# One fixed order for the vector engine's attention work: index sums, choice rounds, scores and rotations queued as traced

## The chip, the cores and the metric

One core of a Trainium2 chip runs the whole program. Its engines each work through an instruction queue of their own, in order: PE (TensorE) for matrix products and transposes, DVE (VectorE) and ACT (ScalarE) for elementwise work, POOL (GpSimd) for a few small vectors, SP (SyncE) for issuing loads. The metric is device time in microseconds (us) of one execution, as the median of several runs.

## The reference

Two layers of a decoder trunk on one sequence of 256 tokens, width 1024, all in float32. Cut to what matters:

```python
for l in range(DEPTH):                               # DEPTH = 2
    mod = c_act @ w_ada[l] + b_ada[l]                # 6 x 1024: shift, scale, gate twice
    sh_m, sc_m, gt_m, sh_f, sc_f, gt_f = split(mod, 6)
    h = rms_norm(x, g_pre_mix[l]) * (1 + sc_m) + sh_m
    # token_mixer: h @ w_in, cut into q|k|v of two head groups, index q|k|weights; partial rotary on q, k
    #   group 1 (MoBA): 8 heads, plain causal attention here (one block of 256 keys)
    #   group 2 (DSA): score[t,s] = sum_h w[t,h] relu(qi[t,h] . ki[s]); the 64 best keys of each
    #                  query are kept, softmax attention over them
    #   each group's output is RMS-normed, then @ w_out
    x = x + gt_m * rms_norm(y, g_post_mix[l])
    h = rms_norm(x, g_pre_ffn[l]) * (1 + sc_f) + sh_f
    y = (gelu(conv3(h @ w_up_act)) * (h @ w_up_lin)) @ w_down
    x = x + gt_f * rms_norm(y, g_post_ffn[l])
```

## The kernel before

Every float32 weight is split on the chip into a high part (ACT, line 141, or 137 with a gain) and the rest (DVE, line 142, or 138), and each product is three passes on PE: high by high, high by rest, rest by high. The 256 tokens are two tiles of 128, called t = 0 and 1. Weights arrive as one stream of 1 MB loads on SP's queue (line 114) into six `raw` buffers, in the order in which the program asks for them.

A layer's mixer projects `ia`, `ib` (index q, index k, index weights), `mq`, `mk`, `mv`, `dq`, `dk`, `dv`, one after the other (lines 380 to 407; layer 0 opens the first four in a common start). While a projection runs, other work is laid between its matrix products by `Background`: chains of generators, each of which is advanced once per step ("tick"); a generator that yields n sleeps for n steps. One projection takes 20 steps: for each t eight, and two more for a pass that is put last (`late`). The chains:

- `T` and `D`: after the rotation of q or k (`rope_out`, lines 353 to 364: a copy on ACT, line 355, then two DVE operations, lines 359 and 364) PE transposes the heads (line 370) and ACT copies them (line 371).
- `att`: `indexer` (lines 415 to 441) multiplies index q by index k, ACT takes the relu (line 433), and DVE adds eight heads up (line 436: an index sum). Then `attend` (lines 457 to 545) for MoBA and, later, DSA: PE makes scores into banks 4 and 5, DVE adds the mask and takes the maximum (line 477: a score operation), ACT takes the exponential with its sum (line 481), DVE the reciprocal (line 484), DVE or ACT the scaling (lines 489, 487), PE transposes (line 496) and multiplies by v.
- `top0`, `top1`: `choose` (lines 443 to 453): eight rounds, each DVE's eight largest of a row (line 447) and their replacement (line 448), with `gap` steps between rounds: 3 in layer 0, 2 in layer 1. The masks that come out are needed by DSA alone.
- `sf`: `gemv_v` (lines 183 to 195): columns of the modulation by DVE, each a row product of 1024 elements with its sum (line 191), two to a load, `gap` steps between two. In layer 0 eight of them (columns 24 to 32) at a gap of 6 start with `mv`, and eight more (columns 32 to 40) at a gap of 9 follow in the same chain, added when `dq` starts.
- `gt`: four-column blocks of the modulation on PE.
- `out`: `group_out` (lines 547 to 567): a norm through PE (line 551), DVE (line 553), POOL (line 555, a power), a transpose on PE (line 558), and two DVE operations (lines 562, 564).

The program's text order is not yet the order of the queues. The framework lays each engine's instructions out at compile time: of those that its own model of the chip holds ready, the one that was traced first. So an instruction traced later may stand earlier in its engine's queue, where the earlier one was not thought ready. `tc.keep_in_program_order` and `tc.issue_after` bind single instructions; nothing of the sort binds those of lines 359, 364, 436, 447, 448 and 477.

Of the kernel before, what the change touches and what calls it, by code (L numbers as in the profile page):

```python
# [14 lines left out]
OP = mybir.AluOpType  # L15
# [11 lines left out]
FILL = -1.0e38  # L27
MARK = -3.0e38
# [46 lines left out]
def trunk(ctx: ExitStack, tc, plan, x, c, stream, small, rope, out):  # L75
    nc = tc.nc
# [7 lines left out]
    bg = Background()  # L84


    def bank(i):
        return ps.tile([128, 512], F32, name=f"b{i}", tag=f"b{i}")
# [17 lines left out]
    st = {"off": 0, "behind": ()}  # L106

    def load(*units, cut=None):


        n = sum(u[3] for u in units)
        t = wts.tile([128, 2048], F32, name="raw", tag="raw", bufs=6)
        for a, b in [(0, cut), (cut, n)] if cut else [(0, n)]:
            nc.sync.dma_start(t[:, a:b], bass.AP(tensor=stream.tensor, offset=stream.offset + st["off"] + a,
                                                 ap=[[n, 128], [1, b - a]]))
        st["off"] += 128 * n
        plan.append(units)
        r, o = [], 0
        for u in units:
            r.append(t[:, o:o + u[3]])  # L120
            o += u[3]
        return r
# [26 lines left out]
    rt = con.tile([128, 2, 2, 16], F32, name="rt")  # L149
# [17 lines left out]
    fill = con.tile([128, 256], F32, name="fill")  # L167
# [11 lines left out]
    def scol(l, name):  # L179
        o = {"b_ada": 0, "g_pre_mix": 48, "g_pre_ffn": 56, "g_post_mix": 64, "g_post_ffn": 72,  # L180
             "g_moba": 80, "g_dsa": 84, "w0": 88, "w1": 110, "w2": 132, "bc": 154}[name]
        return smt[:, l, o:]

    def gemv_v(l, j0, j1, gap, behind=None):

        for j in range(j0, j1, 2):
            r = load(("v_a", l, j, 2048))[0]
            for i in range(2):
                ri = r[:, 1024 * i:1024 * i + 1024]
                with tc.issue_after(behind) if behind else ExitStack():  # L190
                    nc.vector.scalar_tensor_tensor(out=ri, in0=ri, scalar=1.0, in1=crow, op0=OP.mult, op1=OP.mult,  # L191
                                                   accum_out=mods[l][:, j + i:j + i + 1])
                yield gap
        nc.vector.tensor_tensor(out=mods[l][:, j0:j1], in0=mods[l][:, j0:j1],
                                in1=scol(l, "b_ada")[:, j0:j1], op=OP.add)
# [138 lines left out]
    def boundary(ys, g, scale, bias, hh, hl):  # L334
# [15 lines left out]
        p1 = norm_T(1, s1, (6, 4))  # L350
        return a, mod_T(p1, 1, scale, bias, hh, hl)

    def rope_out(p, dst, t, is_q, nh):

        nc.scalar.activation(out=dst, in_=p, func=AF.Copy, scale=0.125 if is_q else 1.0)
        n = wrk.tile([128, 8, 2, 16], F32, name="ra", tag="ra", bufs=2)[:, :nh]
        x = dst[:, :, :16]

        nc.vector.tensor_tensor(out=n, in0=x[:, :, None, :].to_broadcast([128, nh, 2, 16]),
                                in1=rt[:, t][:, None].to_broadcast([128, nh, 2, 16]), op=OP.mult)  # L360
        y = n[:, :, 1]
        y = bass.AP(tensor=y.tensor, offset=y.offset + 8, ap=list(y.ap[:2]) + [[-8, 2], [1, 8]])
        halves = lambda v: v.rearrange("p h (a b) -> p h a b", a=2)
        nc.vector.tensor_tensor(out=halves(x), in0=halves(n[:, :, 0]), in1=y, op=OP.add)

    def heads_T(src, dst, t, wait):
        yield wait
# [40 lines left out]
    def burst(matmuls):  # L408


        for n, (out, lhsT, rhs, flags) in enumerate(matmuls):
            with tc.high_priority() if n else ExitStack():
                ins = nc.tensor.matmul(out, lhsT=lhsT, rhs=rhs, **flags)  # L413
            if n:
                pin(ins)

    def indexer(t, qiT, kiT, wi, res, gap):

        nk = 128 * (t + 1)
        nh = 512 // nk  # L420
        while bg.chains.get("T"):
            yield 1
        sc = wrk.tile([128, 256], F32, name="iscore", tag="iscore", bufs=2)[:, :nk]
        first = True
        for b in range(4 // nh):
            pp = [bank(4), bank(5)]
            burst([(pp[par][:, j * nk:j * nk + nk],
                    qiT[64 * par:64 * par + 64, b * nh + j, 128 * t:128 * t + 128],
                    kiT[64 * par:64 * par + 64, :nk], dict(start=True, stop=True))
                   for j in range(nh) for par in (1, 0)])  # L430
            for par in range(2):
                r = t2()
                nc.scalar.activation(out=r, in_=pp[par], func=AF.Relu)
                for j in range(nh):
                    h = 2 * (b * nh + j) + par
                    nc.vector.scalar_tensor_tensor(out=sc, in0=r[:, j * nk:j * nk + nk], scalar=wi[:, h:h + 1],  # L436
                                                   in1=fill[:, 256 - nk:] if first else sc,
                                                   op0=OP.mult, op1=OP.add)
                    first = False
            yield 3  # L440
        bg.add("top" + str(t), choose(t, nk, sc, res, gap))

    def choose(t, nk, sc, res, gap):

        m8 = tiny(8)
        for _ in range(TOPK // 8):
            nc.vector.max(out=m8, in_=sc)  # L447
            nc.vector.match_replace(out=sc, in_to_replace=m8, in_values=sc, imm_value=MARK)  # L448
            yield gap
        mask = wrk.tile([128, 256], F32, name="mask", tag="mask", bufs=2)[:, :nk]  # L450
        nc.vector.tensor_scalar(out=mask, in0=sc, scalar1=-2.0e38, scalar2=NEG, op0=OP.is_gt, op1=OP.mult)
        nc.vector.tensor_tensor(out=mask, in0=mask, in1=lateneg[:, 256 - nk:], op=OP.min)
        res[t] = mask

    def attend(qT, kT, v, masks, k0, oh, ol, ready):
# [5 lines left out]
        def scores(i):  # L461
            t, b = sets[i]
            nk = 128 * (t + 1)
            nh = 512 // nk
            mask = masks[t] if masks is not None else lateneg[:, 256 - nk:]
            pp = [bank(4 + par).rearrange("p (h k) -> p h k", h=nh) for par in range(2)]
            burst([(pp[par][:, j, :], qT[64 * par:64 * par + 64, b * nh + j, 128 * t:128 * t + 128],
                    kT[64 * par:64 * par + 64, b * nh + j, :nk], dict(start=True, stop=True))
                   for j in range(nh) for par in (1, 0)])
            for par in range(2):  # L470
                pv = pp[par]
                nm = tiny(4)[:, :nh]
                e = t2()
                ev = e.rearrange("p (h k) -> p h k", h=nh)

                for j in range(nh):
                    nc.vector.tensor_tensor_reduce(out=ev[:, j, :], in0=pv[:, j, :], in1=mask, scale=-1.0,
                                                   scalar=-FILL, op0=OP.add, op1=OP.min, accum_out=nm[:, j:j + 1])
                sm = tiny(4)[:, :nh]
                for j in range(nh):  # L480
                    nc.scalar.activation(out=ev[:, j, :], in_=ev[:, j, :], func=AF.Exp, bias=nm[:, j:j + 1],  # L481
                                         scale=-1.0, accum_out=sm[:, j:j + 1])
                rs = wrk.tile([128, 4], F32, name="rs", tag="rs", bufs=4)[:, :nh]
                nc.vector.reciprocal(out=rs, in_=sm)
                if t and (par or masks is None):
                    for j in range(nh):
                        nc.scalar.activation(out=ev[:, j, :], in_=ev[:, j, :], func=AF.Copy, scale=rs[:, j:j + 1])
                else:
                    nc.vector.tensor_tensor(out=ev, in0=ev, in1=rs[:, :, None].to_broadcast([128, nh, nk]), op=OP.mult)
                live[i, par] = [e]  # L490
# [291 lines left out]
    hh, hl, opened, first = start()  # L782

    for l in range(DEPTH):

        qiT = big("qT")
        kiT = wrk.tile([128, S], F32, name="kiT", tag="kiT", bufs=1)
        qs, kis, wis = {}, {}, {}
# [49 lines left out]
            run_project("ib", lambda t, a: idx_out(1, t, a))  # L838
            st["behind"] = placed[0]
        if l == 0:  # L840
            bg.add("sf", gemv_v(l, 24, 32, 6))
            bg.add("gt", gemv_p(l, 16, 24, 34, 16))
        bg.add("gt", gate_rows(l, "mix"))
        if l:
# [1 line left out]
        masks = {}  # L846
# [9 lines left out]
            st["behind"] = ()  # L856
            bg.drain("T")
        for t in range(2):
            bg.add("att", indexer(t, qiT, kiT, wis[t], masks, 2 if l else 3))
        tps["free"] = [6]  # L860
        if l:
            run_project("mk", qk_done(mkT, False))
# [40 lines left out]
        while st["out"] < 2:  # L903
# [4 lines left out]
        first = [[split(raw, "lin" if g < 1 or u < 1 else None) for u, raw in enumerate(load(*us))]  # L908
                 for g, us in enumerate(project_units(l, "lin"))]
# [6 lines left out]
        scale, bias = pre_scale(l, "ffn")  # L916
# [80 lines left out]
        if l + 1 < DEPTH:  # L997
            hh, hl = hT_tiles()
            scale, bias = pre_scale(l + 1, "mix")
# [85 lines left out]
```

## Time and profile before

| | |
|---|---|
| Median of 3 runs | 687.06 us (687.0 to 687.5) |
| The profiled execution: its time | 687.11 us |
| its span in the profile | 685.3 us |
| busy in the span | PE 663.1, DVE 548.5, ACT 425.0, POOL 31.1 us |
| TensorE clock | 0.998 of full speed over the span |

A span is the time from the first to the last instruction that the profile shows; 1.8 us of the execution lie around it. In the timelines each line gives start (us from the span's start), length, engine, line of the kernel, operation, output and input tiles, count, and in brackets how long the engine had stood idle before and what ended that. Matmuls are pipelined: one of 512 columns is shown with 0.39 us, and the next starts 0.23 us after it. DVE instructions overlap a little too.

### The profile page before, as it was taken

The numbers are of one execution on the slowest core, as the hardware profiler recorded it, in microseconds if no ns is written. First come the engines' busy times: TensorE is split into PE (matmuls) and PEld (weight loads), VectorE is DVE, ScalarE is ACT, GpSimd is POOL, SyncE is SP. The second block draws the span as 40 slices with busy tenths as digits, with TensorE's granted clock in tenths as the row PEclk, the third lists the DMA queues.
The fourth block names the chain that finished last, engine by engine and source line by source line (L and its number), as shares of the span: only waits on it lengthen the run. The fifth ranks groups of instructions, "written<-read, shape, count | busy, mean of one in ns | idle before, by whom it ended". The sixth has DMA issues, their size and how long they took to land.

```text
span 685.3 us, 11287 instructions
## 1 busy us (share of the span) xinstructions
PE 663.1 (97%) x4309; PEld 568.6 (83%) x4309; DVE 548.5 (80%) x1088; ACT 425.0 (62%) x788; POOL 31.1 (5%) x57
## 2 busy tenths in 40 slices
PE   7999899998999999999999999999999999999996
PEld 5787676776999999999988677877799999999994
DVE  5898999977999999897689985677689876666553
ACT  6566686976955555555486558878696555555441
POOL 1000002102000000000020000001200000000001
PEclk9999999999999999999999999999999999999999
DMA  8999558963599999997536642446246885545001
GB/s 356 421 412 382 201 219 327 348 221 122 192 361 342 375 379 354 342 328 262 185 124 256 267 148 99 133 175 224 85 184 234 297 329 190 210 185 184 1 1 62
DMA packets 24806, 163.04 MB, mean 238 GB/s; under 512 B 3344, under 2 KB 3760, under 8 KB 6576
## 3 DMA queue, kind: packets, MB, share of 16 engines
q1 hardware_dynamic: 23472, 159.77, 61.8%
q0 software_dynamic: 704, 2.11, 1.0%
q8 instruction: 34, 0.56, 0.3%
q10 hardware_dynamic: 576, 0.43, 0.2%
q14 instruction: 20, 0.16, 0.1%
HBM read 161.24 MB, written 1.06 MB: 237 GB/s over the span
## 4 chain that ended last, share of the span: by engine, by line
PE 75%; DVE 12%; ACT 5%; issue 3%; DMA 2%; POOL 2%; POOLq 0%; DVEq 0%; ACTq 0%
PE b L571 18%; PE b L570 18%; PE b L569 18%; PE b L393 13%; DVE wl L142 3%; PE b L413 2%; DVE iscore L436 2%; DMA raw<-in_stream_dram 2%; PE b L496 1%; DVE iscore L448 1%; ACT t L256 1%; DVE raw L702 1%; PE b L747 1%; DVE tiny L447 1%; ACT t L481 1%
## 5 line engine op out<-in xcount | busy, mean ns | idle before, releaser
L142 DVE TENSOR_TENSOR wl<-raw,wh 128x1024 fp32r<-128x1024 f32 (+1 forms) x146 | 172.5, 1195 | 36.8 <-ACT wh L141 32.8
L569 PE MATMUL b<-hh,wh 128*128 128x256 f32 x640 | 179.9, 281 | 0.0
L571 PE MATMUL b<-hl,wh 128*128 128x256 f32 x640 | 179.6, 281 | 0.0
L570 PE MATMUL b<-hh,wl 128*128 128x256 f32 x640 | 179.6, 281 | 0.0
L141 ACT ACTIVATE wh<-raw 128x1024 fp32r<-128x1024 f32 (+1 forms) x146 | 149.0, 1046 | 48.9 <-PE b L571 35.8
L570 PEld LDWEIGHTS b<-hh,wl 128*128 128x128 f32 x640 | 122.5, 191 | 1.3
L569 PEld LDWEIGHTS b<-hh,wh 128*128 128x128 f32 x640 | 120.2, 188 | 1.5
L571 PEld LDWEIGHTS b<-hl,wh 128*128 128x128 f32 x640 | 120.1, 188 | 0.0
L191 DVE SCALAR_TENSOR_TENSOR raw<-raw,crow 128x1024 f32<-128x1024 f32 x72 | 86.5, 1217 | 1.3 <-DMA raw<-in_stream_dram 1.3
L393 PE MATMUL b<-wh,hh 128*128 128x512 f32 (+1 forms) x184 | 73.5, 402 | 0.1
L393 PE MATMUL b<-wh,hl 128*128 128x512 f32 (+1 forms) x184 | 68.6, 388 | 0.0
L142 DVE TENSOR_TENSOR dl<-raw,dh 128x1024 fp32r<-128x1024 f32 (+2 forms) x47 | 56.8, 1210 | 12.5 <-ACT dh L141 12.5
L141 ACT ACTIVATE dh<-raw 128x1024 fp32r<-128x1024 f32 (+2 forms) x47 | 49.5, 1057 | 25.0 <-PE b L570 25.0
L965 ACT ACTIVATE t<-b,smt 128x256 f32<-128x256 f32 x44 | 25.0, 569 | 56.2 <-PE b L571 56.2
L569 PE MATMUL b<-dh,t 128*128 128x512 f32 x152 | 59.7, 393 | 0.0
L570 PE MATMUL b<-dh,t 128*128 128x512 f32 x152 | 59.6, 392 | 0.0
L571 PE MATMUL b<-dl,t 128*128 128x512 f32 x152 | 59.2, 389 | 0.0
L393 PE MATMUL b<-wl,hh 128*128 128x512 f32 (+1 forms) x184 | 55.0, 390 | 0.0
L393 PEld LDWEIGHTS b<-wh,hh 128*128 128x128 f32 x184 | 34.7, 189 | 9.1 <-issue 2.1
L393 PEld LDWEIGHTS b<-wl,hh 128*128 128x128 f32 x184 | 33.8, 189 | 6.3 <-issue 0.7
L393 PEld LDWEIGHTS b<-wh,hl 128*128 128x128 f32 x184 | 33.8, 189 | 5.9 <-issue 0.5
L966 DVE SCALAR_TENSOR_TENSOR t<-b,smt,t 128x255 f32<-128x255 f32 x44 | 21.1, 480 | 20.5 <-ACT t L965 20.4
(173 smaller groups left out, 1102.2 us busy)
## 6 DMA issues: line engine op xcount, KB each, us to landing
raw<-in_stream_dram SPq DMA_DIRECT2D x142, 1024.0 KB, 6.8
raw<-in_stream_dram SPq DMA_DIRECT2D x7, 804.0 KB, 10.3
gate<-gated POOLq DMA_DIRECT2D x4, 512.0 KB, 8.4
raw<-in_stream_dram SPq DMA_DIRECT2D x3, 512.0 KB, 6.5
xt<-in_x_dram SPq DMA_DIRECT2D x2, 512.0 KB, 4.3
raw<-in_stream_dram SPq DMA_DIRECT2D x1, 984.0 KB, 5.3
out_dram<-xt SPq DMA_DIRECT2D x2, 256.0 KB, 2.1
raw<-in_stream_dram SPq DMA_DIRECT2D x1, 328.0 KB, 5.2
```

The source lines that it names most:

```text
L141: put(nc.scalar.activation(out=hi[:, :n], in_=raw, func=AF.Copy))
L142: put(nc.vector.tensor_tensor(out=lo[:, :n], in0=raw, in1=hi[:, :n].bitcast(F32), op=OP.subtract))
L191: nc.vector.scalar_tensor_tensor(out=ri, in0=ri, scalar=1.0, in1=crow, op0=OP.mult, op1=OP.mult, accum_out=mods[l][:, j + i:j + i + 1])
L256: nc.scalar.activation(out=t2(BF) if to is None else to, in_=src, func=AF.Square, scale=float(n) ** -0.5, accum_out=s)
L393: mm = lambda l_, k, i, start=False, stop=False: nc.tensor.matmul(a[:, :n], lhsT=l_[:, k, tt], rhs=w[k][i], start=start, stop=stop)
L413: ins = nc.tensor.matmul(out, lhsT=lhsT, rhs=rhs, **flags)
L436: nc.vector.scalar_tensor_tensor(out=sc, in0=r[:, j * nk:j * nk + nk], scalar=wi[:, h:h + 1], in1=fill[:, 256 - nk:] if first else sc, op0 ...
L569: nc.tensor.matmul(y, lhsT=hh, rhs=wh, start=first, stop=False)
L570: nc.tensor.matmul(y, lhsT=hl, rhs=wh, start=False, stop=False)
L571: nc.tensor.matmul(y, lhsT=hh, rhs=wl, start=False, stop=last)
L965: nc.scalar.activation(out=z, in_=p[:, :256], func=AF.Identity, scale=w2[:, i:i + 1], bias=bc[:, i:i + 1])
L966: nc.vector.scalar_tensor_tensor(out=z[:, 1:], in0=p[:, :255], scalar=w1[:, i:i + 1], in1=z[:, 1:], op0=OP.mult, op1=OP.add)
```

## The change

```diff
+    def queue(ins):
+        if "last" in st:
+            tc.add_manual_dep(ins.ins, st["last"].name, mybir.DependencyInfo(
+                mybir.DependencyClass.NoSync, mybir.DependencyReason.DATA), reason="queue")
+        st["last"] = ins.ins
+        return ins
...
-        nc.vector.tensor_tensor(out=n, in0=x[:, :, None, :].to_broadcast([128, nh, 2, 16]),
+        queue(nc.vector.tensor_tensor(out=n, in0=x[:, :, None, :].to_broadcast([128, nh, 2, 16]),
...
-        nc.vector.tensor_tensor(out=halves(x), in0=halves(n[:, :, 0]), in1=y, op=OP.add)
+        queue(nc.vector.tensor_tensor(out=halves(x), in0=halves(n[:, :, 0]), in1=y, op=OP.add))
...
-                    nc.vector.scalar_tensor_tensor(out=sc, in0=r[:, j * nk:j * nk + nk], scalar=wi[:, h:h + 1],
+                    queue(nc.vector.scalar_tensor_tensor(out=sc, in0=r[:, j * nk:j * nk + nk], scalar=wi[:, h:h + 1],
...
-            nc.vector.max(out=m8, in_=sc)
-            nc.vector.match_replace(out=sc, in_to_replace=m8, in_values=sc, imm_value=MARK)
+            queue(nc.vector.max(out=m8, in_=sc))
+            queue(nc.vector.match_replace(out=sc, in_to_replace=m8, in_values=sc, imm_value=MARK))
...
-                    nc.vector.tensor_tensor_reduce(out=ev[:, j, :], in0=pv[:, j, :], in1=mask, scale=-1.0,
+                    queue(nc.vector.tensor_tensor_reduce(out=ev[:, j, :], in0=pv[:, j, :], in1=mask, scale=-1.0,
...
-            bg.add("sf", gemv_v(l, 24, 32, 6))
+            bg.add("sf", gemv_v(l, 24, 32, 4))
...
-            bg.add("att", indexer(t, qiT, kiT, wis[t], masks, 2 if l else 3))
+            bg.add("att", indexer(t, qiT, kiT, wis[t], masks, 5 if l else 3))
```

`queue` gives each of these DVE instructions an edge to the one that was traced before it through `queue`, across generators, tiles and layers. The edge is of the class NoSync: it binds the order in which the two are laid into DVE's queue and sets no semaphore. All other DVE instructions (splits, row products, reciprocals, scalings, norms) are laid between them as before. Two gaps change: layer 0's first eight row products come every four steps in place of six, and layer 1's choice rounds every five in place of two. No instruction is added or left out.

## Rows read from the trace of the kernel before

**Rows 1.** The page: busy time of the engines, and DVE's busy share in 40 slices of the span (9 is 90% or more).

```profile
PE 663.1 (97%) x4309; PEld 568.6 (83%) x4309; DVE 548.5 (80%) x1088; ACT 425.0 (62%) x788; POOL 31.1 (5%) x57
DVE  5898999977999999897689985677689876666553
```

**Rows 2.** Busy time of each engine in stretches of the two mixers (stretch, its length, then busy us and instructions of PE, its weight loads, DVE, ACT, POOL, granted clock, DMA share, GB/s).

```profile
67.00:80.00 13.00, 12.55 (x74) 8.88 (x71) 12.13 (x30) 8.86 (x14) 0.00 (x0) 1.00 0.76 281
80.00:100.00 20.00, 18.23 (x140) 12.51 (x139) 19.86 (x81) 16.52 (x46) 0.54 (x1) 1.00 0.41 147
100.00:121.00 21.00, 19.80 (x141) 15.03 (x141) 20.18 (x52) 14.66 (x28) 4.93 (x1) 1.00 0.85 345
...
392.00:406.00 14.00, 12.33 (x58) 10.03 (x59) 13.42 (x43) 6.28 (x9) 0.00 (x0) 1.00 0.43 151
412.00:430.00 18.00, 17.78 (x116) 13.17 (x115) 10.73 (x49) 16.14 (x50) 0.56 (x1) 1.00 0.23 82
```

**Rows 3.** What PE waited for in layer 0's mixer (59 to 150 us), whole us, times, longest; and, after the line of dots, in layer 1's (376 to 480 us).

```profile
PE b L558 <- POOL tiny L555: 1.2, 1, 1.2
PE b L413 <- DVE tiny L477: 1.1, 1, 1.1
PE b L496 <- DVE rs L484: 0.6, 1, 0.6
...
PE b L370 <- ACT wh L141: 1.1, 1, 1.1
PE b L370 <- DVE t L364: 1.1, 2, 0.7
```

**Rows 4.** PE's timeline at the two longest stops of layer 1's mixer.

```profile
391.48 0.40 PE L393 MATMUL b<-wh,hl 128*128 128x512 f32 x1
393.02 0.63 PE L370 MATMUL b<-ident,t 128*128 128x128 f32 x4 [1.15 <-ACT wh L141]
...
398.75 0.40 PE L393 MATMUL b<-wh,hl 128*128 128x512 f32 x1
399.80 0.63 PE L370 MATMUL b<-ident,t 128*128 128x128 f32 x4 [0.65 <-DVE t L364]
```

**Rows 5.** First ACT's copies ahead of the two rotations of those stops, then DVE's timeline up to them and the next four splits.

```profile
389.16 0.60 ACT L355 ACTIVATE t<-b 128x512 f32<-128x512 f32 x1 [1.41 <-PE b L393]
...
396.43 0.60 ACT L355 ACTIVATE t<-b 128x512 f32<-128x512 f32 x1 [0.72 <-PE b L393]
...
391.34 0.62 DVE L447 MAX8 tiny<-iscore 128x8 f32<-128x128 f32 x2
391.87 0.41 DVE L359 TENSOR_TENSOR ra<-t,rt 128x256 f32<-128x256 f32 x1
...
392.59 0.28 DVE L364 TENSOR_TENSOR t<-ra 128x128 f32<-128x128 f32 x1
...
397.18 1.21 DVE L142 TENSOR_TENSOR wl<-raw,wh 128x1024 fp32r<-128x1024 f32 x1
...
398.65 0.40 DVE L359 TENSOR_TENSOR ra<-t,rt 128x256 f32<-128x256 f32 x1
...
399.37 0.28 DVE L364 TENSOR_TENSOR t<-ra 128x128 f32<-128x128 f32 x1
...
407.40 4.63 DVE L142 TENSOR_TENSOR wl<-raw,wh 128x1024 fp32r<-128x1024 f32 x4 [1.85 <-PE b L393]
```

**Rows 6.** A choice round's first operation with an independent one behind it, and with the operation that needs its result behind it (DVE's timeline, layer 1).

```profile
385.90 0.29 DVE L447 MAX8 tiny<-iscore 128x8 f32<-128x128 f32 x1
386.11 0.47 DVE L436 SCALAR_TENSOR_TENSOR iscore<-t,wi,iscore 128x256 f32<-128x256 f32 x1
...
388.12 0.30 DVE L447 MAX8 tiny<-iscore 128x8 f32<-128x128 f32 x1
388.45 0.09 DVE L448 MATCH_VALUE_LOAD iscore<-tiny,iscore 128x8 f32 x1
```

**Rows 7.** Row products, splits and the reciprocal in layer 0's mixer (DVE's timeline).

```profile
64.88 0.08 DVE L191 DVE_READ_ACCUMULATOR raw<-raw,crow 128x1 f32 x1
67.76 2.36 DVE L142 TENSOR_TENSOR wl<-raw,wh 128x1024 fp32r<-128x1024 f32 x2 [2.80 <-ACT wh L141]
...
79.26 1.22 DVE L191 SCALAR_TENSOR_TENSOR raw<-raw,crow 128x1024 f32<-128x1024 f32 x1
...
81.89 1.22 DVE L191 SCALAR_TENSOR_TENSOR raw<-raw,crow 128x1024 f32<-128x1024 f32 x1
...
124.05 1.20 DVE L191 SCALAR_TENSOR_TENSOR raw<-raw,crow 128x1024 f32<-128x1024 f32 x1
```

**Rows 8.** PE's timeline at three stops of layer 0's mixer.

```profile
82.02 1.13 PE L413 MATMUL b<-kT,qT 64*128 64x256 f32 x8 [1.06 <-DVE tiny L477]
...
84.18 0.63 PE L496 MATMUL b<-ident,t 128*128 128x128 f32 x4 [0.60 <-DVE rs L484]
...
129.60 1.09 PE L413 MATMUL b<-t,v 128*64 128x128 f32 x16 [0.23 <-ACT t L498]
```

**Rows 9.** POOL's power of `group_out`, twice, and DVE's work beside the first.

```profile
109.32 4.93 POOL L555 TENSOR_TENSOR tiny<-tiny,mhalf 128x1 f32<-128x1 f32 x1 [16.82 <-DVE tiny L553]
...
135.82 0.56 POOL L555 TENSOR_TENSOR tiny<-tiny,mhalf 128x1 f32<-128x1 f32 x1 [7.09 <-DVE tiny L553]
...
110.03 3.49 DVE L142 TENSOR_TENSOR wl<-raw,wh 128x1024 fp32r<-128x1024 f32 x3
```

More of the change, by code (lines that the diff above doesn't have):

```diff
@@ L357, in rope_out @@
         x = dst[:, :, :16]
-        nc.vector.tensor_tensor(out=n, in0=x[:, :, None, :].to_broadcast([128, nh, 2, 16]),
-                                in1=rt[:, t][:, None].to_broadcast([128, nh, 2, 16]), op=OP.mult)
+        queue(nc.vector.tensor_tensor(out=n, in0=x[:, :, None, :].to_broadcast([128, nh, 2, 16]),
+                                      in1=rt[:, t][:, None].to_broadcast([128, nh, 2, 16]), op=OP.mult))
         y = n[:, :, 1]
@@ L435, in indexer @@
                     h = 2 * (b * nh + j) + par
-                    nc.vector.scalar_tensor_tensor(out=sc, in0=r[:, j * nk:j * nk + nk], scalar=wi[:, h:h + 1],
-                                                   in1=fill[:, 256 - nk:] if first else sc,
-                                                   op0=OP.mult, op1=OP.add)
+                    queue(nc.vector.scalar_tensor_tensor(out=sc, in0=r[:, j * nk:j * nk + nk], scalar=wi[:, h:h + 1],
+                                                       in1=fill[:, 256 - nk:] if first else sc,
+                                                       op0=OP.mult, op1=OP.add))
                     first = False
@@ L476, in scores @@
                 for j in range(nh):
-                    nc.vector.tensor_tensor_reduce(out=ev[:, j, :], in0=pv[:, j, :], in1=mask, scale=-1.0,
-                                                   scalar=-FILL, op0=OP.add, op1=OP.min, accum_out=nm[:, j:j + 1])
+                    queue(nc.vector.tensor_tensor_reduce(out=ev[:, j, :], in0=pv[:, j, :], in1=mask, scale=-1.0,
+                                                       scalar=-FILL, op0=OP.add, op1=OP.min,
+                                                       accum_out=nm[:, j:j + 1]))
                 sm = tiny(4)[:, :nh]
```

## The prediction

> **What bounds the kernel now.** The page comes first: PE is busy for 663.1 of 685.3 us, DVE for 548.5, and DVE's slices reach 9 only in parts [rows 1]. So the end is set by PE's work plus PE's stops, and a change that touches DVE's order alone can only add stops or take some away. The table by stretch says where DVE could make them: from 80 to 121 us (layer 0's mixer) DVE is busy for 40.04 of 41 us, and from 392 to 406 us (layer 1's) for 13.42 of 14, with PE losing 1.67 of those 14 [rows 2]. From 406 us on DVE has room again, 10.73 of 18 us busy between 412 and 430 [rows 2]. PE's waits in the two mixers then name the stops: three in layer 0, of 1.2, 1.1 and 0.6 us, and the transposes of rotated heads in layer 1, 1.1 us once and 1.1 us in two [rows 3]. All of them lie behind DVE or behind POOL. What the change can win is bounded by these: about 5 us together.
>
> One of the names needs care. The stop before 393.02 is put down to a split on ACT [rows 4], but DVE's rotation, which these transposes read, ran from 392.59 to 392.87 [rows 5]: that is the late one.
>
> **The change part by part.**
>
> *Layer 1's rounds, every five steps for two.* At both stops PE holds transposes that wait for line 364, and its next projection products stand behind them in its queue. PE's step for 512 columns is 0.23 us (front, how to read); from the start at 391.48 to the next at 393.02 are 1.54 us, so 1.31 lost, and from 398.75 to 399.80 are 1.05, so 0.82 [rows 4]. ACT had the first head copy ready at 389.76, but DVE began the rotation at 391.87; the second was ready at 397.03 and began at 398.65 [rows 5]. In the 2.1 and 1.6 us between DVE did index sums, rounds, and a split of 1.21 us. At a gap of 2 the eight rounds of t = 0 are traced in 16 steps and those of t = 1 end some six later, nearly all within `mk` (20 steps). At a gap of 5 only rounds 1 and 2 of t = 0 are traced before the first rotation of `mk`, and four of t = 0 with two of t = 1 before the second; in the queue the rest must stand behind the rotations. A round of t = 0 is two operations of some 0.3 us, so three or four rounds less are about 2 us off DVE ahead of the first rotation, as much as it was late: I take the whole 1.31. Ahead of the second the rounds are fewer too, but PE reaches its place 1.3 us sooner, and splits fill what the rounds leave: I take half, 0.4. The deferred rounds, at most ten, do not vanish. They go where DVE stood idle for 1.85 us before 407.40 and into the stretch at 10.73 of 18 [rows 2, 5]. If that cover were gone, the MoBA scores would come later by the rounds still unplayed, and both stops would be lost again: bounds 0 and 2.1 us won, value 1.7. The masks are needed only by DSA, a projection and more later.
>
> *Layer 0's row products, every four steps for six.* Six of the eight stand before the idle 2.80 us that ends at 67.76; the seventh and eighth stand at 79.26 and 81.89, inside the softmax of the first MoBA scores, 1.2 us each [rows 7], and the two stops there, 1.06 and 0.60, wait for line 477 and for the reciprocal behind them [rows 8]. At steps 1 to 29 all eight are traced before `dq` begins, so these two can use the idle 2.80. But the chain `sf` then starts its next eight at `dq`'s first step, at about the steps (34 and 43) where the seventh and eighth had stood (37 and 43). They will be put nearly in the same places, so I count only 0.3 us of the 1.66 as won. The whole chain ends 15 steps earlier instead: two products fewer from 124 us on, where one stood between reciprocal and scaling of the DSA softmax (124.05) [rows 7]. PE stopped for 0.23 us behind that, at 129.60, waiting for ACT [rows 8]: 0.2. The fourth of these loads moves ahead of `dq`'s two on SP's queue, which shifts each of them by one buffer release; `dq`'s splits wait on ACT and PE at that time, not on loads, as the 2.80 us of idle ended by ACT say [rows 7]. Bounds: 1.9 us won (all three stops), 0.6 lost (a product put before the scores where it stood behind them costs half its 1.2 us).
>
> *The queue itself.* The edge sets no semaphore, so it adds no wait on the chip; its cost lies in what it forbids. Before, the compiler laid other work between a round's maximum and its replacement, as at 385.90, where the next instruction began 0.21 us later; where they are neighbours, as at 388.12, it began 0.33 us later [rows 6]. So a dependent pair costs DVE 0.12 us. With both token tiles' rounds in one line, the maximum of one can no longer fill the other's pause; splits and row products may, where ready. There are 16 rounds in each layer, so 0 to 1.9 us of DVE per layer, and somewhat more for index sums. In layer 1 the room after 406 us hides it. In layer 0, 80 to 121 us has no room on DVE, but PE has only these few stops there and splits are ready ahead of the products that read them; of at most 1.9 I count 0.2 against the kernel. A gain is not excluded: scores no longer have a third round ahead of them, some 0.2 us. This is in the 0.3 above. A rotation now stands ahead of scores that are traced later; the copy on ACT that it waits for holds those too, at most some tenths, hidden by ACT's own queue.
>
> The Trainium skill speaks to this in VectorE: DVE Perf Modes, section The DRAIN you can't avoid: the next operation does not start until the pipeline is empty, chained without semaphores or not, so neighbours would cost nothing extra. Rows 6 differ from it (0.21 and 0.33 us), and the measurement decides; by the page the term of 0.2 would be 0 and the time 0.2 us lower.
>
> *Sum.* 1.31 + 0.4 + 0.3 + 0.2 - 0.2 = 2.0 us won. The execution that the profile shows took 687.11 us (span 685.3 and 1.8 around it), 0.05 from the median of the runs. 687.1 - 2.0 = **685.1 us**.
>
> **The rivals.**
>
> *Nothing to measure.* The stops only move. PE arrives 1.3 us sooner at the next place that DVE supplies: the MoBA scores, which stand behind four splits of 4.63 us from 407.40 [rows 5]. For: DVE's total between 376 and 414 us is the same but for what the later rounds take out. Against: the 1.85 us of idle. If the last rounds and the four splits meet, 1.7 is given back, and with 0.2 to 0.4 left in layer 0 the time is 686.8.
>
> *The queue starves layer 0 (slower).* The place is DVE from 67 to 121 us, 52.2 of 54 us busy [rows 2]. The price is 16 x 0.12 = 1.9 us for rounds and 8 x 0.12 = 1.0 for index sums that were laid alternately, 2.9 us. It decides from the point where the splits of `dv`, three in a row from 110.03 [rows 9], end later than PE asks for them: their pass is not put last, and PE had already stopped 1.2 us there. Of 2.9 us some 2.3 would then reach PE, with 1.0 lost by pulled row products at the scores and 1.7 won in layer 1: 687.1 + 1.6 = 688.7.
>
> *More than forecast.* POOL's power took 4.93 us from 109.32, and 0.56 at 135.82; beside the long one DVE ran three splits back to back [rows 9], and PE's stop of 1.2 us is the transpose that reads it [rows 3]. If the new order leaves DVE a pause or other work there, 1.2 goes, and if the row products leave the scores too, 1.4 more of rows 8: 685.1 - 2.6 = 682.5.
>
> The Trainium skill, SBUF — State Buffer, section Who interferes with whom, has a DVE instruction with two SBUF inputs contend with a GpSimd instruction that reads SBUF. Rows 9 agree (splits read `raw` and `wh`). By that rule any new run of such splits beside line 555 makes a stop of this kind, and any break in one removes it.
>
> *It does not do what it says.* Most tied instructions already stand in traced order, and the gap matters little because the compiler draws rounds forward whenever DVE looks idle: 687.0.
>
> **How the numbers follow.** Forecast 0.44, its own range 683.8 to 686.4; nothing to measure 0.14; starved 0.22; more 0.12; not what it says 0.08. A tenth part of the forecast's own chance falls above the bound below. What a measurement of this kernel tells from no change is about 0.2%, 1.4 us: faster is below 685.7, slower above 688.4. Faster: 0.40 of the forecast and 0.12, 0.52. Slower: the starved case but for its mild end, 0.20, and 0.02 for what I have not seen. Same: the rest, 0.26. The range reaches to 682.2 for the case of more and to 688.9 for the starved one.
>
> **What would show it.** Right: no stop over 0.3 us at the transposes of `mk` (line 370 after 390 us), rounds spread to beyond 410 us, all first eight row products before 68 us, the last of the next eight before 121 us. Wrong: a stop at the MoBA scores near 412 us as long as those removed; DVE pauses of 0.1 us between neighbours with PE stopped behind `dv`'s splits near 113 us; a longer POOL power; or rounds of layer 1 as dense as before.

## The result, and the profile after

| | before | after |
|---|---|---|
| median | 687.12 us (686.72 to 687.5, 6 runs) | 691.06 us (690.54 to 692.08, 6 runs) |
| ratio | 1 | 1.0059, 95% interval 1.0048 to 1.0069 |
| span in the profile | 685.3 us | 688.9 us (execution 690.72) |

The change makes the kernel 3.9 us slower; forecast were 2.0 us won, and the time lies above the range too. In `after` every line from 355 on has moved: 355 is 363, 359/364 are 367/372, 370 is 378, 413 is 421, 433/436 are 441/444, 447/448 are 455/456, 477 is 485, 484/489 are 493/498, 496 is 505, 498 is 507 (ACT's copy of the transposed softmax), 524 is 533, 551 is 560, 555/558 are 564/567.

The page of after, which answers to [rows 1]: PE's work is what it was, DVE has 3.9 us more, POOL 4.4 less.

```profile
PE 663.8 (96%) x4309; PEld 568.9 (83%) x4309; DVE 552.4 (80%) x1088; ACT 424.6 (62%) x788; POOL 26.7 (4%) x57
...
DVE  5899999877899999898679996677689976666553
```

The same products of PE, compared between the two traces, say where the time goes: a projection product at 54.44 us before is at 54.18 after; the one at 158.12 is at 161.44; the one at 354.27 at 357.59; the one at 517.56 at 521.15. So 3.6 us are lost in layer 0's mixer, nothing between the mixers, and 0.3 in layer 1's. Busy time by stretch, as in [rows 2]:

```profile
80.00:100.00 20.00, 16.40 (x93) 11.33 (x95) 19.53 (x74) 13.18 (x37) 0.30 (x1) 1.00 0.51 179
100.00:121.00 21.00, 20.21 (x175) 14.42 (x176) 18.54 (x53) 16.52 (x34) 0.90 (x2) 1.00 0.68 253
```

From 80 to 100 us PE is busy for 16.40 us where it was 18.23. And DVE, which had no room there, is busy for 18.54 us between 100 and 121 us where it was 20.18: late and idle at once. What PE waited for from 59 to 150 us, against [rows 3]:

```profile
PE b L421 <- DVE tiny L485: 1.5, 1, 1.5
PE b L505 <- DVE t L498: 1.2, 1, 1.2
PE b L421 <- ACT t L441: 1.2, 1, 1.2
PE b L421 <- ACT t L507: 1.0, 2, 0.7
PE b L505 <- DVE rs L493: 0.7, 1, 0.7
```

5.6 us where the three rows of before are 2.9. POOL's 1.2 is gone; the wait for MoBA's scores (L485) has grown, the one for DVE's scaling behind them (L498) is new, and two that were 0.3 and 0.2 us before have grown to 1.2 and 1.0: the wait of the index products (index q by index k) for ACT's relu (L441), and that of the products with v for ACT's copy (L507). How DVE comes to be late stands in its timeline between MoBA's first group of scores (the last of its eight at 83.60) and its second:

```profile
84.41 0.42 DVE L455 MAX8 tiny<-iscore 128x8 f32<-128x256 f32 x1
84.74 1.21 DVE L191 SCALAR_TENSOR_TENSOR raw<-raw,crow 128x1024 f32<-128x1024 f32 x1
...
86.01 0.41 DVE L456 MATCH_REPLACE8 iscore<-tiny,iscore 128x256 f32<-128x256 f32 x1
...
87.02 1.19 DVE L191 SCALAR_TENSOR_TENSOR raw<-raw,crow 128x1024 f32<-128x1024 f32 x1
...
89.40 1.23 DVE L142 TENSOR_TENSOR wl<-raw,wh 128x1024 fp32r<-128x1024 f32 x1 [0.24 <-ACT wh L141]
...
90.74 0.29 DVE L455 MAX8 tiny<-iscore 128x8 f32<-128x128 f32 x1
90.95 1.21 DVE L142 TENSOR_TENSOR wl<-raw,wh 128x1024 fp32r<-128x1024 f32 x1
92.07 0.09 DVE L456 MATCH_VALUE_LOAD iscore<-tiny,iscore 128x8 f32 x1
...
92.34 0.42 DVE L455 MAX8 tiny<-iscore 128x8 f32<-128x256 f32 x1
92.67 1.21 DVE L142 TENSOR_TENSOR wl<-raw,wh 128x1024 fp32r<-128x1024 f32 x1
93.79 0.09 DVE L456 MATCH_VALUE_LOAD iscore<-tiny,iscore 128x8 f32 x1
...
94.19 0.42 DVE L485 CUSTOM_DVE_ANT_0 t<-b,lateneg 128x256 f32<-128x256 f32 x1
```

Read each maximum (L455) with what comes behind it: not its replacement and not the other tile's maximum, but a split or a row product of 1.2 us, after which the round goes on. Five instructions of that length stand between the two groups: three inside rounds (84.74, 90.95, 92.67), one ahead of a scaling (87.02) and one inside a rotation (89.40). In the kernel before there is one (81.89 in [rows 7]), and what follows its maxima there is short, a scaling, a rotation, a score:

```profile
84.05 0.39 DVE L447 MAX8 tiny<-iscore 128x8 f32<-128x256 f32 x1
84.36 0.67 DVE L489 TENSOR_TENSOR t<-t,rs 128x512 f32<-128x512 f32 x1
...
85.68 0.28 DVE L447 MAX8 tiny<-iscore 128x8 f32<-128x128 f32 x1
85.89 0.27 DVE L364 TENSOR_TENSOR t<-ra 128x128 f32<-128x128 f32 x1
...
86.34 0.41 DVE L447 MAX8 tiny<-iscore 128x8 f32<-128x256 f32 x1
86.67 0.40 DVE L477 CUSTOM_DVE_ANT_0 t<-b,lateneg 128x256 f32<-128x256 f32 x1
```

The last row opens the second group of before.

### The profile page after: what moved, and what is told of

The parts are those of the page before. It is cut to its first block, busy times and chain, and to the rows that moved or that the text cites. A ratio compares the mean times of both kernels' runs of the same rounds, so it can differ in the third digit from the quotient of the medians.

```text
span 688.9 us, 11277 instructions
## 1 busy us (share of the span) xinstructions
PE 663.8 (96%) x4309; PEld 568.9 (83%) x4309; DVE 552.4 (80%) x1088; ACT 424.6 (62%) x788; POOL 26.7 (4%) x57
## 4 chain that ended last, share of the span: by engine, by line
PE 72%; DVE 14%; ACT 7%; issue 3%; DMA 2%; POOL 1%; POOLq 0%; DVEq 0%; ACTq 0%
PE b L580 18%; PE b L578 18%; PE b L579 18%; PE b L401 11%; DVE wl L142 4%; PE b L421 2%; DMA raw<-in_stream_dram 2%; DVE iscore L444 2%; ACT t L490 1%; PE b L505 1%; DVE iscore L456 1%; DVE raw L191 1%; ACT t L256 1%; DVE raw L711 1%; PE b L756 1%
```

## The experiments

All kernels do the whole computation, and each is compared with runs of the kernel before on the same chip. "Second group" is the start of MoBA's second group of scores in layer 0 in the profiled execution (before: 86.67), and n the number of 1.2 us instructions of DVE from the first index sum to it (before: 4).

**The change taken apart.** First the queue alone, then each gap alone, then queue and row products. Edits to the changed kernel:

```diff
 e1: both gaps as before (only queue() stays)
 e2: no queue, layer 1's gap 2           e3: no queue, row products every 6
 e4: queue and row products every 4, layer 1's gap 2
 e1, e2 and e4:
-            bg.add("att", indexer(t, qiT, kiT, wis[t], masks, 5 if l else 3))
+            bg.add("att", indexer(t, qiT, kiT, wis[t], masks, 2 if l else 3))
 e1 and e3:
-            bg.add("sf", gemv_v(l, 24, 32, 4))
+            bg.add("sf", gemv_v(l, 24, 32, 6))
```

The queue alone. 

> The one queue alone, both gaps as before (row products every six steps, layer 1's rounds every two). Theory A (the queue itself delays layer 0's first scores: index sums of t = 1 stand single file behind those of t = 0, and splits and row products fill the places between): 3 to 4 us slower than before, and PE stops at the first MoBA scores and transposes of layer 0 of 3 us or more together. Theory B (the earlier row products are the cost, since the next eight then stand ahead of the scores): within 1 us of before.

Row products alone. 

> The row products every four steps alone, no queue, rounds every two. Theory A: within 1 us of before, perhaps some tenths faster. Theory B: 3 to 4 us slower, with two row products of the second eight between the index sums of layer 0 and the first scores late by 2.3 us or more.

Layer 1's rounds alone. 

> Layer 1's rounds every five steps alone. Both theories put the loss in layer 0, so nothing of it here. The forecast's term for layer 1 was 1.7 us won; the changed kernel's trace shows layer 1 no better than before at its end. If the rounds' spacing does win and the queue gives it back: 1 to 2 us faster than before. If the stops only move: within 0.5 us.

Queue and row products. 

> The queue and the early row products, rounds of layer 1 every two as before. Theory A: as slow as the queue alone, 3 to 4 us. Theory B: as slow as the row products alone. If the two only cost together (row products fill the places that the queue leaves): this is 3 to 4 us slower while both alone are within 1 us.

Measured (before: 687.22): e1 690.69, ratio 1.0047 (1.0032 to 1.0062); e2 686.96, 0.9998 (0.9989 to 1.0007); e3 686.81, 0.9990 (0.9981 to 1.0000); e4 691.21, 1.0057 (1.0042 to 1.0072). The queue is the whole loss, and each gap by itself is worth nothing that can be measured. Theory A has the size right and the stops in part: PE in e1 stops 1.5 us at the first scores and 0.4 at the transposes behind them, and another 1.6 at a projection product that waits for ACT's split (line 401). Row products every four steps only move stops. From PE's waits of e2, 59 to 150 us:

```profile
PE b L413 <- ACT t L433: 1.2, 1, 1.2
...
PE b L551 <- DVE ss L524: 1.1, 2, 0.8
```

The first was 0.3 before and the second is new in this stretch; in return POOL's stop of 1.2 us is gone. In e3, without the queue, the transposes in layer 1 lose what they lost before [rows 3]; the spacing is not kept:

```profile
PE b L370 <- ACT wh L141: 1.2, 1, 1.2
PE b L370 <- DVE t L364: 1.0, 2, 0.5
```

**Which part of the queue.** Edits to e1 (gaps as before); e8 is the whole queue in layer 1 alone, at a gap of 5.

```diff
 e5: queue() left off index sums, scores and rotations   e6: queue() left off maxima and replacements
 e7: queue(..., t), one line per token tile
-        if "last" in st:
+        if ("last", t) in st:
 e8: layer 1 alone
+        if l != 1:
+            return ins
```

> Only the maxima and replacements are tied (index sums, scores and rotations free, both gaps as before). Theory P (pauses): between a tied maximum and its replacement lies a pause of about 0.1 us, the other tile's round may not fill it, and the compiler lays a split or a row product of 1.2 us there; every round behind it, and the masks with them, come later, and PE is made to wait. In this order 8 of layer 0's 16 rounds have one, so P expects most of the 3.5 us of the whole queue: 688.7 to 690.7. Theory S (scores): the cost is made where MoBA's first scores stand behind index sums in single file and behind row products drawn forward (PE stops 1.5 us at line 421 and 0.7 to 1.2 behind). Here the scores stand as in the kernel before, so S expects 686.7 to 687.6, no stop at line 421 over 1.1 us.

> Index sums, scores and rotations are tied, the rounds are free (both gaps as before). Theory P: no pause of a round is filled by a 1.2 us instruction (1 of 16), so the time is that of the kernel before, 686.7 to 687.8, although the scores still stand behind the index sums. Theory S: first score after 81 us as with the whole queue, PE stop of about 1.5 us there, 689.3 to 690.7.

> The same four kinds are tied, but in two lines, one for each token tile, so that the two tiles' rounds may fill each other's pauses (2 of 16 rounds with a 1.2 us instruction inside, both gaps as before). Theory P: 686.7 to 687.8. Theory S: the scores of tile 0 no longer stand behind the index sums of tile 1, so it too expects the cost to go, 686.7 to 687.8. If a third thing makes the cost, such as rotations that hold the rounds behind them while ACT copies (2.1 us of idle before a rotation at 104.4 us in the changed kernel), this stays at 688.5 or more.

> The queue holds in layer 1 alone, with its rounds every five steps; layer 0 is as before. All theories: layer 0's loss of 3.3 us goes. By the waits of the runs so far layer 1's transposes of rotated heads lose 1.6 us in place of 2.2, and scaling reads another 0.5 to 1.0 more: 686.3 to 687.5. By the prediction's term for layer 1 (1.7 won) 685.4.

Measured (before: 686.99): e5 686.02, ratio 0.9993 (0.9984 to 1.0001); e6 686.03, 0.9991 (0.9982 to 1.0000); e7 686.41, 0.9999 (0.9991 to 1.0008); e8 687.11, 1.0007 (0.9998 to 1.0016). Theory P falls as it was put: with the rounds alone tied, 8 of 16 in layer 0 have a 1.2 us instruction inside, and nothing is lost, for the scores pass them (second group at 86.41). Theory S falls too: with everything but the rounds tied the first scores do come later (80.71, before 79.05), and nothing is lost. It takes rounds and something else in one line; with a line for each tile the time is that of before (second group at 87.23). And e8 shows that layer 1 wins nothing.

**Rounds with which other kind.** Edits to e1: `queue()` left off one kind at a time. The fourth run, e12, combines e6's layer 0 with the queue in layer 1 at a gap of 4.

> Index sums, rounds and scores tied, rotations free, both gaps as before. The runs so far: rounds alone tied cost nothing (686.0), the three other kinds tied without rounds cost nothing (686.0), all four cost 3.5. So the cost belongs to rounds together with one other kind. Theory I (rounds and index sums): the sums of tile 1 may not be laid between the rounds of tile 0, both then run neighbour behind neighbour with row products laid into the pauses, and MoBA's first scores, which PE waits for, come 2 us later: 689.5 to 691. Theory R (rounds and rotations): a rotation that waits for ACT's copy holds the rounds behind it, 686 to 687.5. Theory M (rounds and scores): scores hold rounds and the masks come late, 689 to 691.

> Rounds, scores and rotations tied, index sums free, both gaps as before. Theory I: 686 to 687.5, the first score at about 79 us on the trace as in the kernel before. Theory R and theory M: 689 to 691.

> Index sums, rounds and rotations tied, scores free, both gaps as before. Theory I: the scores may now be laid between sums and rounds, which takes away the stop at line 421 but not the lateness of the sums: between 687 and 690. Theory R: 689 to 691. Theory M: 686 to 687.5.

> Meant as a version that beats both: layer 0 as in the run with the rounds free (686.0), layer 1 with the whole queue and a gap of 4, so that all rounds are done ahead of MoBA's scores (at a gap of 5 the last round stood among them, and PE lost 0.9 us behind the reciprocal, line 505). If that stop goes (0.9) and the rotations' win of the gap of 5 (0.7) stays at least in half, 685.0 to 685.6; if the rounds drawn forward delay the rotations instead, 685.9 to 686.5.

Measured (before: 686.94): e9 690.41, ratio 1.0044 (1.0029 to 1.0059); e10 689.34, 1.0033 (1.0023 to 1.0043); e11 687.45, 1.0009 (1.0000 to 1.0018); e12 685.96, 0.9991 (0.9982 to 1.0000). Theory R falls: without rotations in the line nearly all of the loss is there. Theory I explains a third at most (690.69 to 689.34; e1's two executions at a mean clock of 0.997 and 0.999 took 689.90 and 690.45, see the last section). Without the scores most of it goes, which speaks for M, that scores stand behind rounds. The stop that e12 was to remove, 0.7 us at line 505's place in layer 1, went, and 0.4 came at the scores there.

**Order or pauses.** Whether M's pair is enough, whether the order alone does it, and whether fewer rounds ahead help. Edits to e1:

```diff
 e13: queue() left off index sums and rotations
 e14:
-            queue(nc.vector.max(out=m8, in_=sc))
+            nc.vector.max(out=m8, in_=sc)
 e15:
-            bg.add("att", indexer(t, qiT, kiT, wis[t], masks, 2 if l else 3))
+            bg.add("att", indexer(t, qiT, kiT, wis[t], masks, 2 if l else 6))
```

> Only rounds and scores are tied; index sums and rotations free, both gaps as before. Theory M (the second token tile's scores stand behind the rounds traced before them, so PE, which waits for each group's softmax, runs late) holds for this pair alone: second group of scores at 91 us or later on the trace, 688.5 to 690. If the cost needs a third kind (index sums or rotations) in the line as well, 686 to 687.5 with the second group before 89 us.

> The whole queue but for the maxima: of each round only the replacement is tied, so that the other tile's maximum may fill the pause before it, while the order of rounds and scores is the same as with the whole queue. 3 of 16 rounds have a 1.2 us instruction inside instead of 12. Theory P+ (the scores stand behind the rounds, and what makes that dear is the pauses filled with splits and row products): second group before 91 us, 687 to 688.7. Theory O (the order alone makes the cost, pauses or not): second group at 93 to 94 us, 689.7 to 691.

> The whole queue, with layer 0's rounds every six steps for three (row products every six and layer 1's rounds every two steps as before). Fewer rounds are traced ahead of the second and third group of scores (2 for 7 ahead of the second in the compiled order). Both theories: second group at 89 to 92 us. Masks come later and DSA's first scores, 10 us after, may then wait for them: if they do not, 687 to 689; if they do, 689.5 to 692, with the stop moved to line 421 near 125 us.

Measured (before: 686.97): e13 685.78, ratio 0.9990 (0.9980 to 1.0000); e14 686.91, 1.0001 (0.9991 to 1.0010); e15 689.29, 1.0039 (1.0025 to 1.0053). So M's pair alone does not lose: its second group comes at 89.60, and that is early enough. e14 is the run that decides: replacements, index sums, scores and rotations all stay in the line, only the maxima leave it, and 3.8 us come back. Its DVE timeline behind the first scores shows why:

```profile
83.58 0.61 DVE L455 MAX8 tiny<-iscore 128x8 f32<-128x128 f32 x2
...
84.24 0.28 DVE L456 MATCH_REPLACE8 iscore<-tiny,iscore 128x128 f32<-128x128 f32 x1
...
85.10 0.41 DVE L456 MATCH_REPLACE8 iscore<-tiny,iscore 128x256 f32<-128x256 f32 x1
85.43 0.28 DVE L455 MAX8 tiny<-iscore 128x8 f32<-128x128 f32 x1
...
85.70 0.40 DVE L455 MAX8 tiny<-iscore 128x8 f32<-128x256 f32 x1
...
87.02 1.22 DVE L191 SCALAR_TENSOR_TENSOR raw<-raw,crow 128x1024 f32<-128x1024 f32 x1
...
88.44 0.27 DVE L456 MATCH_REPLACE8 iscore<-tiny,iscore 128x128 f32<-128x128 f32 x1
...
89.03 0.41 DVE L485 CUSTOM_DVE_ANT_0 t<-b,lateneg 128x256 f32<-128x256 f32 x1
```

Both tiles' maxima stand ahead of both replacements (the first row is two of them): one fills the other's pause. In the first pair of rounds no long instruction is laid there, in the second one row product for both tiles (87.02). P+ holds and O falls. In e15 the second group came at 88.99, as expected, and the loss moved to DSA: the deferred rounds run until 123.6 us there, the first DSA scores begin at 125.10 (before 121.92), and PE stops behind them:

```profile
132.33 0.66 PE L505 MATMUL b<-ident,t 128*128 128x128 f32 x4 [0.60 <-DVE t L498]
...
146.65 0.65 PE L505 MATMUL b<-ident,t 128*128 128x128 f32 x4 [1.12 <-DVE ss L533]
```

**The whole change but for the maxima, and the kernel before once more.** The first edit is e14's, made to the changed kernel.

> The whole change (queue, row products every four steps, layer 1's rounds every five) with the maxima alone left out of the queue. If the tied maxima make the whole loss, the 4 us go: 686 to 687.5, second group of scores in layer 0 before 91 us. If row products forward and spaced rounds matter beside the queue, 688 or more. Layer 1's win at the rotations (0.7) should again be given back behind the reciprocal at line 505, since the last round still stands among MoBA's scores.

> The kernel before, unchanged, to see a second profiled execution of it. Its times so far fall into two groups, 685.4 to 686.1 and 686.7 to 688.5. If POOL's power at line 555, which took 4.93 us in the first profile, makes the difference (PE's stop of 1.2 us at line 551), then a profile with a time below 686.2 shows it at 1.7 us or less and no such stop, and one above 686.7 shows it at 4 to 5 us again.

Measured (before: 687.07): e16 687.45, ratio 1.0008 (0.9998 to 1.0017); e17 687.10, 1.0001 (0.9992 to 1.0011), profiled at 687.00 (PE's stop behind the power is at line 558, not 551). One word leaves the change, and its loss goes from 3.9 us to one that can't be told from none. The profiled execution of e16 is one of three long ones (688.87 to 689.03; the other seven took 687.24 to 687.52); what makes it long lies in layer 0 (last section), so below its trace serves for layer 1.

The runs side by side (n, second and third group in us, time):

```
                               n   second  third   time
before                         4   86.67   97.86   687.1
e5  rounds only                4   86.41   97.35   686.0
e7  two lines                  4   87.23   98.21   686.4
e11 scores free                5   87.95   98.33   687.5
e6  rounds free                5   88.54  100.39   686.0
e14 maxima free                5   89.03  100.36   686.9
e13 rounds and scores only     6   89.60   98.61   685.8
e9  rotations free             7   91.72  103.76   690.4
e10 index sums free            8   91.84  102.79   689.3
e1  queue alone                9   94.06  106.80   690.7
changed kernel                11   94.19  105.06   691.1
```

(In the changed kernel the index sums begin 2.5 us earlier, so two of its eleven cost nothing.) Each long instruction let in moves the second group by 1.3 to 2.4 us, with the shorter work that comes along. Up to 89.6 us, 2.9 later than before, PE has projection products to do in the meantime; from 91.7 on it loses 2.4 us or more. e15 is left out, since its loss stands at DSA; e4, with the changed kernel's order on DVE in layer 0, fits (11, 94.54, 105.39, 691.2). The loss goes with n and not with how many rounds are filled: of 16 rounds in layer 0, 8 have a 1.2 us instruction inside in e5, e11 and e13, which lose nothing or little, 8 in e10, 7 in e9, 12 in e1 and 6 in the changed kernel, which lose.

Two limits of the table. The step is not sharp: e13's second group is two scores at 89.60 and two from 91.43 on, and e11 is slower than e13 although its group begins earlier. And "nothing lost" is a balance: the kernel before has a stop of 1.2 us behind POOL's power in both its profiles that none of the other kernels of this table has (last section). Against the executions of before that seem to escape it (685.4 to 686.1), e5, e6 and e13 cost 0.3 us at most, e7 0.7, e14 1.2, e11 1.8 and e1 about 5.

## Why the prediction was wrong

*The bound* was right: PE's work is unchanged, and nearly the whole difference is stops behind DVE's order. The place named as without room on DVE, 80 to 121 us, is where it was lost.

*The queue, 0.2 us against: this step failed*, and it alone turns the sign. It priced a pause at the 0.12 us of [rows 6] and let splits and row products fill it, "where ready", as a gain. The size of the pause was right: in after a maximum with its replacement behind it takes 0.32 us (81.53 to 81.85). But what is laid into 0.12 us is 1.2 us long, the round waits for that, and with index sums or rotations and the scores in the same line PE waits too. Before, short instructions were at hand, a rotation, a score, the other tile's maximum; the one line forbade those, and leaving the maxima alone out of it was enough (e14). The Trainium skill's VectorE: DVE Perf Modes, section The DRAIN you can't avoid, has the next operation start only when the pipeline is empty, chained by semaphores or not. It also says that a next operation that is not held starts earlier, which the prediction left out. Read without that, the term would be 0; [rows 6] show that a dependent neighbour does start 0.12 us later, and the runs show that what is laid there is what costs. Measured in place of 0.2: 3.5 us net alone (e1), 0 net without the maxima (e14), each with POOL's stop of 1.2 us won.

"A rotation now stands ahead of scores ... at most some tenths" was low as well. In after DVE stands still with the third group of scores behind it:

```profile
104.39 0.42 DVE L367 TENSOR_TENSOR ra<-t,rt 128x256 f32<-128x256 f32 x1 [2.06 <-ACT t L363]
```

What that costs by itself is small: e9, without rotations in the line, is at 690.41 for 690.69. So ACT's queue did not hide the wait, as forecast, but it decided nothing.

*The rival "starved"* had the side and two fifths of the price. It counted 0.12 us per pair (688.7) and put the deciding place at `dv`'s splits, 110 to 113 us; 3.4 of the 5.6 us of stops lay more than 20 us earlier, between 82 and 89 us, where scores met rounds. And it bought off 1.7 us with layer 1.

*Layer 1's rounds, 1.7 us won: the term measured 0.* The steps at the rotations were right in kind: with the queue, a gap of 5 takes their waits from 2.9 us (e1) to 1.6 (after), from 2.2 before. PE's two stops of [rows 4] are shorter, not gone; of after:

```profile
395.73 0.63 PE L378 MATMUL b<-ident,t 128*128 128x128 f32 x4 [0.63 <-DVE t L372]
402.57 0.63 PE L378 MATMUL b<-ident,t 128*128 128x128 f32 x4 [0.48 <-DVE t L372]
...
418.88 0.63 PE L505 MATMUL b<-ident,t 128*128 128x128 f32 x4 [0.74 <-DVE rs L493]
```

By PE's progress 0.7 us are won at the first two and 0.9 lost at the third. The failed step is "they go where DVE stood idle": one round of tile 1 went behind MoBA's first scores and ahead of their reciprocal, and its mask with it:

```profile
416.19 0.42 DVE L455 MAX8 tiny<-iscore 128x8 f32<-128x256 f32 x1
...
417.17 0.29 DVE L459 TENSOR_SCALAR mask<-iscore 128x256 f32<-128x256 f32 x1
417.49 0.43 DVE L460 TENSOR_TENSOR mask<-mask,lateneg 128x256 f32<-128x256 f32 x1
417.83 0.17 DVE L493 RECIPROCAL rs<-tiny 128x4 f32<-128x4 f32 x1
```

1.64 us from 416.19 to 417.83, and PE waits for that reciprocal. The bound of 0 for this case was named, with the rule that the last rounds meet the scores; the rival "nothing to measure" had it for layer 1 (e8). With the maxima out of the line the term is not nothing: in e16's profile PE wins 1.2 us at the first two stops and gives 0.7 back at the third, and its layer 1 as a whole is 0.7 us shorter than before. That is one execution, and against e16's expectation, which had the win given back.

*Row products, 0.5 us won: the term measured 0.* All of the first eight ran before 68 us, as forecast. But there they delayed the index sums, and PE stopped 1.2 us at the index products (68.63), 0.3 before; the next eight took the old places at the scores, as the prediction had it, and the last of them ran at 122.92, not before 121.

*"More than forecast"* came true in its first half, unseen in the sum: POOL's power beside `dv`'s splits took 0.66 us in after, and the stop of 1.2 went. So the new order cost layer 0 about 1.2 us more than the 3.6 that remain.

*"Does not do what it says"* was right for the spacing alone (e3) and wrong for the queue, which held the traced order.

What stays open: which of PE's small stops from 100 to 150 us belong to which late score. No run holds the whole order with its pauses left empty, so what the order costs with nothing laid between is not shown; e14, where little is, puts it near 1.2 us in place of 5. That e10 loses a third less than e9 at the same second group fits the granted clock (last section): e9's three executions at a mean clock of 0.995 or 0.996 took 690.41 to 690.58 us, its two at 0.998 took 688.97 and 689.93, about e10's 688.25 to 689.91.

## What to carry to other kernels

An edge that only orders a queue still has a price: what it forbids is replaced by whatever is left, and that price is the length of the replacement, not of the pause. Before tying instructions that run in dependent pairs, look in the timeline at what fills the pairs' pauses now, and leave the first of each pair free or give each independent strand its own line. And a change of several parts is judged by its parts and by their combinations: here rounds alone (e5), all but the rounds (e6) and rounds with scores (e13) were no slower than the kernel before, and three kinds with the rounds among them lost 0.5 to 3.5 us.

## What the runs showed of the hardware

**One collision, two times.** The runs of the kernel before fall into two groups with nothing between: beside e5 to e8, 12 of 33 took 685.51 to 686.12 us and 21 took 686.82 to 688.21. How many are in the lower group differs: 1 of 19 beside e1 to e4, none of 19 beside e16 and e17. POOL's power on one element per partition tells them apart, as far as profiles go. e17, at 687.00, and e8, at 686.06, whose order on DVE in layer 0 is the same (its line 566 is 555):

```profile
109.09 4.93 POOL L555 TENSOR_TENSOR tiny<-tiny,mhalf 128x1 f32<-128x1 f32 x1 [16.82 <-DVE tiny L553]
...
109.80 3.49 DVE L142 TENSOR_TENSOR wl<-raw,wh 128x1024 fp32r<-128x1024 f32 x3
...
114.44 0.69 DVE L562 TENSOR_TENSOR o<-o,b 128x512 f32<-128x512 f32 x1 [0.81 <-PE b L558]
```

```profile
109.40 0.66 POOL L566 TENSOR_TENSOR tiny<-tiny,mhalf 128x1 f32<-128x1 f32 x1 [16.81 <-DVE tiny L564]
...
110.11 3.48 DVE L142 TENSOR_TENSOR wl<-raw,wh 128x1024 fp32r<-128x1024 f32 x3
```

In both the splits begin 0.71 us after the power. Where the power ends in 0.66 it is through 0.05 us before them; where it isn't, it takes 4.93, 0.7 us beyond the end of the splits, and PE's transpose waits. The Trainium skill (SBUF — State Buffer, section Who interferes with whom) has such splits, with two SBUF inputs, contend with a GpSimd instruction that reads SBUF. e17 agrees, and in e8 the power escapes by a hair. All runs of e6 and e12, in whose profiles no power of that stretch took over 1.46 us, lie between 685.79 and 686.35. That is about 1 us below the median of the kernel before and no lower than its lower group: what they win is, it seems, the collision. Only profiled executions show the power's length, so for the other runs this is inferred from their times.

**In some executions the clock fell as well.** In the profiled executions of e1, e9 and e16 the granted TensorE clock fell below full between 80 and 100 us, after PE had been busy for 6.5 to 6.9 of 10 us. In after, at 6.57 of 10, and in e4, at 6.59, it did not, so a thin stretch alone does not decide it. First e1, then e16:

```profile
80.00:90.00 10.00, 6.50 (x31) 4.41 (x31) 10.00 (x40) 6.16 (x20) 0.00 (x0) 0.93 0.42 129
90.00:100.00 10.00, 10.00 (x55) 7.38 (x54) 9.38 (x33) 7.13 (x17) 0.00 (x0) 0.90 0.71 249
```

```profile
80.00:90.00 10.00, 6.91 (x34) 4.67 (x33) 9.86 (x49) 5.85 (x21) 0.00 (x0) 0.97 0.24 95
90.00:100.00 10.00, 10.00 (x81) 6.63 (x80) 8.54 (x29) 8.33 (x19) 1.46 (x1) 0.86 0.18 48
```

Full is the level of 2.4 GHz; the other is 1.2. In e1 the two stretches of 10 us fall short of full by 0.07 and 0.10, in e16 by 0.03 and 0.14: by estimate up to 1.7 us of PE's work in either case, which no stop shows. The mean granted clock of every run is on record and fits: e16's three long runs, 1.6 us above its others, are the three at 0.995, the others at 0.997 to 0.999. Of the changed kernel's six runs the two longest (691.76 and 692.08) are at 0.995, the other four at 0.997 or 0.998. The kernel before is not free of it: its profiles show 1.00 throughout this stretch, but all eight of the runs beside the experiments that took over 688 us are at 0.996.
